# Sums of squares, products with M and scores later in TensorE's order, and a block's end as a chain of its own beside the next block's fetches

## The chip, the cores and the metric

The kernel runs on one core of a Trainium2 chip. Its engines are TensorE (PE; its weight loads are listed as PEld), VectorE (DVE), ScalarE (ACT), GpSimd (POOL), and SyncE (SP), whose work here is to issue DMAs. Each engine runs its own list of instructions in order and waits on semaphores for the others. The metric is the time of one execution on the device in microseconds (us), lower is better.

## The reference

One encoder layer over 1024 tokens of width 1024, float32, one sequence:

```
h   = modulate(rmsnorm(x))                      # scales and shifts from c
mix = gated sum of attention(h) and ssd(h)      # two token mixers, then w_out
x   = x + g1 * mix
h   = modulate(rmsnorm(x))
x   = x + g2 * peer(h)
out = rmsnorm(x) * final_norm_w
```

`ssd` is a state-space mixer in both directions, in chunks of 128 tokens, 16 heads in 2 groups. Per chunk and group its output is `M @ X` (M: 128x128 for each head, a masked product of B and C with decays) plus decayed products with the states of the chunks before (forward) and behind (backward), plus a skip term, times silu(z), followed by an rmsnorm over all 1024 channels, which needs the sum of squares of every token.

`peer` has 16384 experts. For each of 8 heads a query gives scores against two sets of 128 keys; the 16 best of each make 256 pairs, of which the 16 best are kept:

```
s1, s2 = q1 @ keys1.T, q2 @ keys2.T             # 128 scores each
idx, g = the 16 best of the 256 sums, softmax   # 8 x 16 = 128 experts per token
a      = gelu(u[idx] . h)                       # 128 rows of u for each token
y      = sum over the 128 of (g * a) * v[idx]
```

## The kernel before, in words

**The stages.** In the order of time: modulation and the first norm, the input projection, attention, the SSD mixer (its outputs from 691 to 1043 us), the gates and w_out, the second norm, the PEER queries and scores (scores from 1290 us), and from there to the end PEER itself. Matrix products are made in three passes with operands split into a high and a low part (`mm3`, lines 209 to 211): a weight slab is loaded by SP (`wr`, 3 buffers), ACT casts the high part (`wh`), POOL or DVE subtracts for the low part (`wl`), 4 buffers each.

**SSD outputs.** `outputs(c, ...)` runs for chunk c = 0 to 7, with g = 0, 1 inside. Each group goes: R matmuls (L802), exp on ACT (E), M on POOL and DVE (L806, L809, L811), the products of x with M into `y` (L815), the products dec that spread the decays over the heads (L820), those of the states (L830), DVE's sum of it all into `yt` (L832 to L843), the Square on ACT (L845), and four matmuls against ones that add the squares over channels into a bank `oq` (L849, each split into four by row in the trace). `cu`, from which M is built, lies in the same bank as `oq`. `step(FSTEP)` then issues pieces of independent projection work (matmuls of `w`), the filler between groups.

**Scores.** For each of 16 half-queries m, `query` makes q for the first 384 tokens, ACT copies it out of PSUM (L1083), and `score` multiplies it with the keys (L1093); `top` picks the 16 best on DVE.

**PEER.** The first 384 tokens (three blocks of 128) take the route by fetches: `fetched()`, a generator, yields "u" for each of 128 fetches of rows of u (POOL issues them, L1282; DVE makes the dot product with the block's rows in the double bank `gx`, L1314), then "v" for each of 128 fetches of v, which PE adds up in `gx` (L1361). `ahead` holds back the work of a fetch for some slots. The other 640 tokens take the dense route: hidden values for all experts (`hb`, weights uT), a one-hot table of the routing weights, G, built by DVE (`quad`, L1478) and PE (L1493) in pages of 64 tokens that SP stores to memory (`G_d`), then, from 2523 us, the mixing: groups of hidden values weighed with G (L1686 to L1692), multiplied with v, added to `acc` by DVE (L1722). The bank rotation `P1()` has four turns, three in `pb` and one in `io`. `gx` is one buffer (`wide()`).

**What sets the order.** In the PEER part the order of PE, DVE and POOL is written out by the program. A planner counts up estimated PE, DVE and DMA time (`at_pe`, `at_dve`, `at_dma`); after each job `feed()` steps the generator until the DMA time has caught up, and it stops at once where the generator yields "w". In the other stages a scheduler orders PE, ACT and SP by estimated times. SP's one queue issues all plain DMAs in order.

**A block's end before.** `finish` and `final` run in the generator: copy `gx` to `bacc`, take `gx` again, eight transposes into it, load x1 (512 KB) into a second `bacc` tile, of which there is one buffer, so that the load waits for the transposes; eight DVE steps (L1252), four pairs of squares on ACT (L1260) with sums on PE into `gx` (L216), the reciprocal root on DVE (L222 to L228), its spread over partitions (L237), eight DVE steps (L1271), the store. 17 times it yields "w" on the way. Only then does the next block's `begin` get `gx`.

Of the kernel before, what the change touches and what calls it, by code (L numbers as in the profile page):

```python
# [124 lines left out]
def block(ctx, tc, A, out, dbg=None):  # L125
# [490 lines left out]
    def C1():  # L616
        return psC.tile([128, 512], F32, name="pb", bufs=4 - NW)
# [149 lines left out]
    def outputs(c, xc, xk, Sf):  # L767
# [22 lines left out]
        for g in range(2):  # L790
# [9 lines left out]
            for j in range(2):  # L800
                for i, (w, r) in enumerate(R):
                    PE.matmul(o[:, j], lhsT=w, rhs=r[:, 4 * j:4 * j + 4], start=(i == 0), stop=(i == 3))  # L802
            E = ss.tile([128, 8, 128], F32, name="E")
# [8 lines left out]
            y = C1()  # L812
            for r in range(8):
                h = 8 * g + r
                PE.matmul(y[64 * (r % 2):64 * (r % 2) + 64, (r // 2) * 128:(r // 2 + 1) * 128],  # L815
                          lhsT=xk[:, h * 64:(h + 1) * 64], rhs=M[:, r], start=True, stop=True, skip_group_check=True)
# [9 lines left out]
            for d in dirs:  # L826
                st = (Sf, Sb)[d]
                for j in range(4):
                    hs = slice((8 * g + 2 * j) * 64, (8 * g + 2 * j + 2) * 64)
                    PE.matmul(of[:, d, j * 128:(j + 1) * 128], lhsT=st[:, hs], rhs=xc[:, 10 + g],  # L830
                              start=True, stop=True, skip_group_check=True)
            V.tensor_tensor(de[:, ds], of[:, ds], de[:, ds], op=OP.mult)  # L832
# [8 lines left out]
            zt = ss.tile([128, 4, 128], F32, name="zt")  # L841
# [4 lines left out]
            if g == 0:  # L846
                qr = slice(32 * (c // 2), 32 * (c // 2) + 32)
            for j in range(4):
                PE.matmul(oq[qr, :128], lhsT=one[:, 0:32], rhs=zt[:, j], start=(g == 0 and j == 0),  # L849
                          stop=(g == 1 and j == 3))  # L850
            step(FSTEP)
        ACT.copy(ysum[qr, (c % 2) * 128:(c % 2) * 128 + 128], oq[qr, :128])
# [12 lines left out]
    for c in range(8):  # L865
        xc, xk = tokens(c)
        outputs(c, xc, xk, Sf)
        if c < 7:
            Sf = advance(Sf, states(c, 0, xc, xk), c, 0)
    step(10 ** 6)  # L870
# [238 lines left out]

    norm = normed(ends[1], accs[1])  # L1110
# [127 lines left out]
    def final(p, src, t0, n, x1):  # L1238
        tl = slice(t0, t0 + n)
        def of(m):  # L1240
            o = src[:, m // 4, m % 4]
            return o if n == 128 else o.rearrange("p (g i) -> p g i", g=4)[:, :, :n // 4]

        def like(ap):
            return ap if n == 128 else ap.rearrange("p (g i) -> p g i", g=4)

        nc.sync.dma_start(x1, x1_d[:, :, tl])
        yield "w"
        yield "w"
        yield "w"  # L1250
        for m in range(8):
            V.scalar_tensor_tensor(like(x1[:, m]), of(m), mod[:, 40 + m:41 + m], like(x1[:, m]), op0=OP.mult, op1=OP.add)  # L1252
        yield "w"
        o = wide()
        acc = o[:, 0]
        for m in range(0, 8, 2):
            some = []
            for _ in range(2):
                some.append(p.tile([128, 128], F32, name="fsq", bufs=2)[:, :n])
                ACT.activation(some[-1], x1[:, m + len(some) - 1], AF.Square)  # L1260
            yield "w"
            for i, sq in enumerate(some):
                sums(sq, acc, n, m + i == 0, m + i == 7)
        yield "w"
        r = rstd(p, acc, n, 1.0 / D)
        yield "w"
        yield "w"
        yield "w"
        rb = rbcast(o[:, 1], r, n)
        for m in range(8):  # L1270
            V.scalar_tensor_tensor(x1[:, m], x1[:, m], cols[:, C_FN + m:C_FN + m + 1], rb, op0=OP.mult, op1=OP.mult)  # L1271
        nc.sync.dma_start(out[:, :, tl], x1)

    def fetched():
# [15 lines left out]
        for b in range(NB):  # L1290
            assert b in ready
            a = rt.tile([128, 128], F32, name="ba", bufs=2)
# [47 lines left out]
            for s in range(slots):  # L1340
# [5 lines left out]
                yield "u"  # L1346
            ahead.append((0, weights_of))
# [18 lines left out]
            def finish(b=b, acc=acc, n=4 * steps):  # L1366
                s = rt.tile([128, D], F32, name="bacc")
                yield "w"
                ACT.copy(v2(s), acc[0])
                yield "w"  # L1370
                yield "w"
                o = wide().rearrange("p s (m t) -> p s m t", m=4)
                for m in range(8):
                    PE.transpose(o[:, m // 4, m % 4], s[:, m * 128:(m + 1) * 128], ident)
                x1 = rt.tile([128, 1024], F32, name="bacc")[:, :8 * n].rearrange("p (m t) -> p m t", m=8)
                yield from final(rt, o, b * 128, n, x1)
# [10 lines left out]
        while ahead:  # L1387
            yield from ahead.pop(0)[1]()

# [477 lines left out]
```

## Time and profile before

| what | value |
|---|---|
| runs | 3956.99, 3949.39, 3957.73 us; median 3956.99 |
| profiled execution | 3962.2 us, its span 3960.4 us, mean granted clock 0.963 |
| busy | PE 92%, PEld 81%, DVE 65%, POOL 46%, ACT 34% of the span |
| DMA | 852.32 MB, mean 215 GB/s |
| the chain that ended last | PE 24%, DVE 5%, DMA 4% of the span, the rest in smaller shares |

The page lists the busy time of each engine, then the span in 40 slices with the busy tenths of each engine and the granted clock of PE (9: 90% or more). Waits are listed as engine, tile and line, then for whom it waited: total us, times, the longest. A line of a group names engine, operation, tile and shape, with count, busy us and mean ns behind the bar's left side, and the idle time before it with its releaser at the end. The block ends lie at about 2206 to 2310 us (block 0, while G is being placed) and 3000 to 3065 us (block 1, beside the mixing).

### The profile page before, as it was taken

The page shows a single profiled execution, that of the slowest core. Times are in us where ns is not written, and L with a number is a line of the kernel's source. Part 1 is how long each engine was busy: PE and PEld are TensorE (multiplying, and loading weights), DVE is VectorE, ACT ScalarE, POOL GpSimd, SP SyncE. Part 2 cuts the span into 40 slices and gives each one's busy share as a digit, 9 for nine tenths or more (in the row PEclk, how much of TensorE's full clock was granted, in tenths as well). Part 3 has the DMA queues.
Part 4 walks back from the last instruction along what each step waited for, and adds up shares of the span by engine and source line. Part 5 has one row for each costly group of instructions (what it writes and reads, how often), then busy time and mean ns, then how long its engine had stood idle before and what let it go on. Part 6 is the DMA issues. An engine that isn't in the chain of part 4 may idle for free. (4 is left out here: it accounts for less than half of the span.)

```text
span 3960.4 us, 61117 instructions
## 1 busy us (share of the span) xinstructions
PE 3631.6 (92%) x22927; PEld 3189.8 (81%) x22927; DVE 2574.5 (65%) x5289; ACT 1356.3 (34%) x2672; POOL 1803.3 (46%) x1526
## 2 busy tenths in 40 slices
PE   7999999988889899999889798699999999999998
PEld 4777767766679799987678698697888999888997
DVE  5788831457672678787875567594447898545556
ACT  5455532223323433322236465222122222222222
POOL 3111122566454567778775456444443444444200
PEclk9999999998899999999999899799999999999999
DMA  5111134233375258877767778888887888888632
GB/s 197 47 46 48 55 117 144 92 106 101 122 241 168 94 201 317 311 284 258 244 231 273 264 265 320 310 300 303 322 323 246 295 297 292 310 317 314 236 117 81
DMA packets 387064, 852.32 MB, mean 215 GB/s; under 512 B 32720, under 2 KB 146896, under 8 KB 384080
## 3 DMA queue, kind: packets, MB, share of 16 engines
q1 hardware_dynamic: 276176, 445.72, 32.9%
q0 software_dynamic: 110592, 402.70, 28.7%
q8 instruction: 180, 2.95, 0.3%
q14 instruction: 116, 0.95, 0.1%
HBM read 739.70 MB, written 108.59 MB: 214 GB/s over the span
## 5 line engine op out<-in xcount | busy, mean ns | idle before, releaser
L209 PE MATMUL hb<-ah,wh 128*128 128x320 f32 x2048 | 653.2, 319 | 24.0 <-ACT a L1459 24.0
L211 PE MATMUL hb<-ah,wl 128*128 128x320 f32 x2048 | 641.1, 313 | 9.7 <-POOL wl L199 9.7
L210 PE MATMUL hb<-al,wh 128*128 128x320 f32 x2048 | 639.9, 312 | 0.0
L1282 POOL DMA_INDIRECT br<-u,bidx x384 | 370.3, 964 | 369.0 <-DVE br L1314 243.2
L199 POOL TENSOR_TENSOR wl<-wr,wh 128x512 fp32r<-128x512 f32 x269 | 352.9, 1317 | 397.3 <-ACT wh L198 367.6
L209 PE MATMUL pb<-Wh,vh 128*128 128x320 f32 x1536 | 477.1, 317 | 57.1 <-ACT Wh L1689 33.7
L180 POOL TENSOR_TENSOR wl<-wr,wh 128x512 fp32r<-128x512 f32 x172 | 233.0, 1358 | 615.5 <-ACT wh L179 450.6
L1282 POOL DMA_INDIRECT br<-v,ixt x384 | 376.8, 981 | 267.5 <-PE gx L1361 155.1
L210 PE MATMUL pb<-Wl,vh 128*128 128x320 f32 x1536 | 481.4, 314 | 1.7 <-DVE Wl L1692 1.6
L211 PE MATMUL pb<-Wh,vl 128*128 128x320 f32 x1536 | 479.6, 313 | 0.0
L1314 DVE SCALAR_TENSOR_TENSOR br<-br,gx 128x1024 f32<-128x1024 f32 x384 | 454.0, 1214 | 8.6 <-DMA br<-u,bidx 6.3
L209 PEld LDWEIGHTS hb<-ah,wh 128*128 128x128 f32 x2048 | 391.9, 191 | 52.7 <-ACT a L1459 28.2
L211 PEld LDWEIGHTS hb<-ah,wl 128*128 128x128 f32 x2048 | 390.7, 191 | 11.3 <-POOL wl L199 10.3
L210 PEld LDWEIGHTS hb<-al,wh 128*128 128x128 f32 x2048 | 391.5, 191 | 0.0
L1722 DVE TENSOR_TENSOR acc<-acc,pb 128x320 f32<-128x320 f32 x491 | 230.6, 485 | 222.2 <-PE pb L211 221.0
L179 ACT CAST vh<-vr 128x512 fp32r<-128x512 f32 x256 | 151.1, 618 | 649.8 <-PE pb L210 449.0
L209 PEld LDWEIGHTS pb<-Wh,vh 128*128 128x128 f32 x1536 | 289.6, 190 | 84.4 <-ACT Wh L1689 37.0
L198 ACT CAST wh<-wr 128x512 fp32r<-128x512 f32 x288 | 178.2, 619 | 397.8 <-PE hb L210 188.2
L210 PEld LDWEIGHTS pb<-Wl,vh 128*128 128x128 f32 x1536 | 292.5, 190 | 5.4 <-DVE Wl L1692 4.3
L211 PEld LDWEIGHTS pb<-Wh,vl 128*128 128x128 f32 x1536 | 292.9, 191 | 0.4
L1478 DVE TENSOR_TENSOR quad<-io,rig 128x1024 f32<-128x1024 f32 x160 | 191.7, 1221 | 139.1 <-PE pb L1493 78.0
L180 DVE TENSOR_TENSOR vl<-vr,vh 128x512 fp32r<-128x512 f32 x256 | 203.9, 797 | 76.8 <-ACT vh L179 76.8
(367 smaller groups left out, 8218.4 us busy)
## 6 DMA issues: line engine op xcount, KB each, us to landing
wr<-uT SPq DMA_DIRECT2D x256, 256.0 KB, 3.9
vr<-v SPq DMA_DIRECT2D x256, 256.0 KB, 5.3
G_d<-stg SPq DMA_DIRECT2D x20, 2048.0 KB, 11.7
gt<-G_d SPq DMA_DIRECT2D x42, 960.0 KB, 6.5
a_d<-a SPq DMA_DIRECT2D x85, 320.0 KB, 5.3
a<-a_d SPq DMA_DIRECT2D x85, 320.0 KB, 5.9
wr<-wi SPq DMA_DIRECT2D x84, 256.0 KB, 2.7
sq<-adaT SPq DMA_DIRECT2D x32, 512.0 KB, 3.8
```

Of the source, the lines that this page charges most:

```text
L179: ACT.copy(hi, src)
L180: (eng or POOL).tensor_tensor(lo, src, f32(hi), op=OP.subtract)
L198: ACT.copy(h, raw)
L199: late.append(lambda: (eng or POOL).tensor_tensor(w, raw, f32(h), op=OP.subtract))
L209: PE.matmul(o, lhsT=wh, rhs=xh, start=first, stop=False)
L210: PE.matmul(o, lhsT=wh, rhs=xl, start=False, stop=False)
L211: PE.matmul(o, lhsT=wl, rhs=xh, start=False, stop=last)
L1282: POOL.indirect_dma_start(out=r, out_offset=None, in_=A[tab], in_offset=bass.IndirectOffsetOnAxis(ap=idx, axis=0))
L1314: V.scalar_tensor_tensor(v2(r), v2(r), 1.0, hrow[0], op0=OP.mult, op1=OP.mult, accum_out=a[:, s:s + 1])
L1478: V.tensor_tensor(x, iota.unsqueeze(1).unsqueeze(1).to_broadcast([128, 2, 4, 128]), ig[:, 0:2, t:t + 4].unsqueeze(3).to_broadcast([128, 2, ...
L1722: V.tensor_tensor(acc[:, m, js], acc[:, m, js], o, op=OP.add)
```

## The change

Four things are moved.

1. The sums of squares. After the Square on ACT, `outputs` only notes (oq, c, g, zt) in a list; `add_squares` makes the matmuls after the R matmuls of the next group, the last ones after the loop. The tile `zt` gets a second buffer. The copy of the sums moves along.
2. The products with M (`y`) come after those of dec and of the states.
3. The score of query m comes after query m+1, with its selection.
4. A block's end. `finish` copies `gx` to `bacc` and appends a generator `tail` to a list; no "w" is yielded. `tail` goes on by one piece at every third "u" of the next block, and in the last block's case at the end with a "w" each. It takes banks from `P1()` and not `gx`; x1 is loaded in two halves into `bx1`, one buffer that the squares use too; eight squares of 128x128 become two of 128x512. `ba` goes from two buffers to one.

```diff
@@ outputs @@
                     PE.matmul(o[:, j], lhsT=w, rhs=r[:, 4 * j:4 * j + 4], start=(i == 0), stop=(i == 3))
+            if squares_of:
+                add_squares()
             E = ss.tile([128, 8, 128], F32, name="E")
...
             V.tensor_tensor(M, M, E, op=OP.mult)
-            y = C1()
-            for r in range(8):
-                h = 8 * g + r
-                PE.matmul(y[...], lhsT=xk[:, h * 64:(h + 1) * 64], rhs=M[:, r], start=True, stop=True, skip_group_check=True)
             od = C2()
...
+            y = C1()
+            for r in range(8):
+                h = 8 * g + r
+                PE.matmul(y[...], lhsT=xk[:, h * 64:(h + 1) * 64], rhs=M[:, r], start=True, stop=True, skip_group_check=True)
             V.tensor_tensor(de[:, ds], of[:, ds], de[:, ds], op=OP.mult)
...
-            zt = ss.tile([128, 4, 128], F32, name="zt")
+            zt = ss.tile([128, 4, 128], F32, name="zt", bufs=2)
...
             ACT.activation(zt, yt, AF.Square)
-            if g == 0:
-                qr = slice(32 * (c // 2), 32 * (c // 2) + 32)
-            for j in range(4):
-                PE.matmul(oq[qr, :128], lhsT=one[:, 0:32], rhs=zt[:, j], start=(g == 0 and j == 0),
-                          stop=(g == 1 and j == 3))
+            squares_of.append((oq, c, g, zt))
             step(FSTEP)
-        ACT.copy(ysum[qr, (c % 2) * 128:(c % 2) * 128 + 128], oq[qr, :128])
+
+    squares_of = []
+
+    def add_squares():
+        oq, c, g, zt = squares_of.pop(0)
+        qr = slice(32 * (c // 2), 32 * (c // 2) + 32)
+        for j in range(4):
+            PE.matmul(oq[qr, :128], lhsT=one[:, 0:32], rhs=zt[:, j], start=(g == 0 and j == 0),
+                      stop=(g == 1 and j == 3))
+        if g:
+            ACT.copy(ysum[qr, (c % 2) * 128:(c % 2) * 128 + 128], oq[qr, :128])
@@ scores @@
-        s = score(m, q, range(NB))
-        for b in range(NB):
-            top(m, s[:, b], b)
+        if m:
+            tops_of(m - 1, q0)
+        q0 = q
+    tops_of(15, q0)
@@ a block's end @@
+    def half_of(b, k):
+        x = rt.tile([128, 4, 128], F32, name="bx1")
+        nc.sync.dma_start(x, x1_d[:, 4 * k:4 * k + 4, 128 * b:128 * b + 128])
+        return x
+
+    def tail(b, s, x1):
+        for k in range(2):
+            o = P1()
+            for m in range(4):
+                PE.transpose(o[:, 128 * m:128 * m + 128], s[:, 512 * k + 128 * m:512 * k + 128 * m + 128], ident)
+            for m in range(4):
+                V.scalar_tensor_tensor(s[:, 512 * k + 128 * m:512 * k + 128 * m + 128], o[:, 128 * m:128 * m + 128],
+                                       mod[:, 40 + 4 * k + m:41 + 4 * k + m], x1[:, m], op0=OP.mult, op1=OP.add)
+            if k == 0:
+                x1 = half_of(b, 1)
+            yield
+        sq = rt.tile([128, 4, 128], F32, name="bx1")
+        ACT.activation(sq.rearrange("p m t -> p (m t)"), s[:, 0:512], AF.Square)
+        yield
+        o = P1()
+        for k in range(2):
+            if k:
+                sq = rt.tile([128, 4, 128], F32, name="bx1")
+                ACT.activation(sq.rearrange("p m t -> p (m t)"), s[:, 512:1024], AF.Square)
+            for m in range(4):
+                sums(sq[:, m], o, 128, k == 0 and m == 0, k == 1 and m == 3)
+        r = rstd(rt, o, 128, 1.0 / D)
+        yield
+        rb = rbcast(P1(), r, 128)
...
+    def go_on():
+        if tails and next(tails[0], 0) == 0:
+            tails.pop(0)
...
                 yield "u"
+                if s % 3 == 2:
+                    go_on()
...
             def finish(b=b, acc=acc):
                 s = rt.tile([128, D], F32, name="bacc")
                 ACT.copy(v2(s), acc[0])
-                ...
+                tails.append(tail(b, s, half_of(b, 0)))
```

How the order moves, at three places. First TensorE in the SSD outputs, group 0 of chunk 1 and the opening of group 1 (`w` is the filler, `St` and `Sb` the forward and backward states, `kb` the spreading matrix); before:

```order
L802 MATMUL pa<-r1l,mr 128x512
L820 MATMUL pa<-dec,kb 128x128 [waits Activation_49]
L830 MATMUL pa<-xc,St 128x128 [waits Activation_49]
L815 MATMUL pb<-M,xk 64x128 [waits DVE_49]
L830 MATMUL pa<-xc,Sb 128x128 [waits DMAHW3_49]
L209 MATMUL w<-hh,wh 128x512
...
L849 MATMUL pb<-zt,ka 32x128 [waits Activation_49]
L802 MATMUL pa<-r0h,mr 128x512 [waits PE_49,Pool_49]
```

and now, up to the first products of group 1:

```order
L802 MATMUL pa<-r1l,mr 128x512
L857 MATMUL pb<-zt,ka 32x128
L817 MATMUL pa<-dec,kb 128x128 [waits Activation_49]
L827 MATMUL pa<-xc,St 128x128 [waits Activation_49]
L827 MATMUL pa<-xc,Sb 128x128 [waits DMAHW4_49]
L832 MATMUL pb<-M,xk 64x128 [waits DVE_49]
L209 MATMUL w<-hh,wh 128x512
...
L802 MATMUL pa<-r0h,mr 128x512 [waits Activation_49,Pool_49]
...
L857 MATMUL pb<-zt,ka 32x128 x4
L817 MATMUL pa<-dec,kb 128x128 [waits DVE_49]
```

The squares of group 0 (L849, now L857) stood behind the 24 filler matmuls and stand behind those and the eight R matmuls (L802); the products with M (L815, now L832) stood among those of the states and stand behind them.

Second, POOL at block 0's end, where fetches of u for block 1 (`br<-u`) meet the low parts of weights (`wl`) and the multiplication of one-hot tables (`quad`); before:

```order
L199 TENSOR_TENSOR wl<-wr,wh 128x512 [waits DMAHW1_49,PE_49,Activation_49]
L1484 TENSOR_TENSOR quad<-quad,rig 128x512 [waits DVE_49] x2
L1282 DMA br<-u,bidx 128x1024 [waits DMASW7_49]
L1282 DMA br<-u,bidx 128x1024 [waits DMASW0_49]
L1282 DMA br<-u,bidx 128x1024 [waits DMAHW3_49,DMASW1_49,Activation_49]
L1282 DMA br<-u,bidx 128x1024 [waits DMASW2_49,DVE_49]
...
L1282 DMA br<-u,bidx 128x1024 [waits DMASW5_49,DVE_49]
L199 TENSOR_TENSOR wl<-wr,wh 128x512 [waits DMAHW2_49,PE_49]
L199 TENSOR_TENSOR wl<-wr,wh 128x512 [waits DMAHW4_49,PE_49,Activation_49]
```

and now:

```order
L1503 TENSOR_TENSOR quad<-quad,rig 128x512 [waits DVE_49]
L1301 DMA br<-u,bidx 128x1024 [waits DMASW7_49]
L1301 DMA br<-u,bidx 128x1024 [waits DMASW0_49]
L199 TENSOR_TENSOR wl<-wr,wh 128x512 [waits DMAHW0_49,PE_49,Activation_49]
L199 TENSOR_TENSOR wl<-wr,wh 128x512 [waits PE_49,DMAHW2_49,Activation_49,Pool_49]
L1503 TENSOR_TENSOR quad<-quad,rig 128x512 [waits DVE_49] x2
L1301 DMA br<-u,bidx 128x1024 [waits DMAHW4_49,DMASW1_49]
L1301 DMA br<-u,bidx 128x1024 [waits DMASW2_49]
L199 TENSOR_TENSOR wl<-wr,wh 128x512 [waits DMAHW3_49,PE_49,Activation_49]
```

Before, 15 fetches stood one behind the other ahead of the next low part; now they come two at a time.

Third, DVE at the same place, where block 0's end (`bacc`) meets the one-hot tables and the dots of block 1 (`br,ba<-br,gx`); before:

```order
L1478 TENSOR_TENSOR quad<-io,rig 128x1024 [waits PE_49,Pool_49] x2
L1252 SCALAR_TENSOR_TENSOR bacc<-gx,mod,bacc 128x128 [waits DMAHW7_49]
L1478 TENSOR_TENSOR quad<-io,rig 128x1024 [waits DVE_49,PE_49,Activation_49] x2
L1478 TENSOR_TENSOR quad<-io,rig 128x1024 [waits PE_49,Pool_49]
L222 TENSOR_SCALAR rstd_32_20404<-gx 128x32 [waits PE_49]
...
L1271 SCALAR_TENSOR_TENSOR bacc<-bacc,cols,gx 128x128 [waits PE_49]
L1314 SCALAR_TENSOR_TENSOR br,ba<-br,gx 128x1024 [waits DMASW3_49,DMASW5_49,DMASW1_49,DMASW7_49,DMASW0_49,Activation_49]
```

and now:

```order
L1333 SCALAR_TENSOR_TENSOR br,ba<-br,gx 128x1024 [waits DMASW5_49,DMASW3_49,DMASW7_49,DMASW1_49,DMASW0_49]
L1497 TENSOR_TENSOR quad<-io,rig 128x1024 [waits DVE_49,PE_49,Activation_49]
L1497 TENSOR_TENSOR quad<-io,rig 128x1024 [waits PE_49,Pool_49] x2
L1266 SCALAR_TENSOR_TENSOR bacc<-pb,mod,bx_20216 128x128 [waits PE_49]
L1333 SCALAR_TENSOR_TENSOR br,ba<-br,gx 128x1024 [waits DMASW4_49,DMASW6_49,DMASW2_49,DMASW1_49]
...
L1333 SCALAR_TENSOR_TENSOR br,ba<-br,gx 128x1024 [waits DMASW3_49]
L1266 SCALAR_TENSOR_TENSOR bacc<-pb,mod,bx_20318 128x128 [waits DMAHW7_49,PE_49]
```

The dots of block 1 began behind the whole of block 0's end and now begin ahead of its first step; the steps of the end stand one set at a time between dots and one-hot tables.

More of the change, by code (lines that the diff above doesn't have):

```diff
@@ L811, in outputs @@
             V.tensor_tensor(M, M, E, op=OP.mult)
-            y = C1()
-            for r in range(8):
-                h = 8 * g + r
-                PE.matmul(y[64 * (r % 2):64 * (r % 2) + 64, (r // 2) * 128:(r // 2 + 1) * 128],
-                          lhsT=xk[:, h * 64:(h + 1) * 64], rhs=M[:, r], start=True, stop=True, skip_group_check=True)
             od = C2()
@@ L831, in outputs @@
                               start=True, stop=True, skip_group_check=True)
+            y = C1()
+            for r in range(8):
+                h = 8 * g + r
+                PE.matmul(y[64 * (r % 2):64 * (r % 2) + 64, (r // 2) * 128:(r // 2 + 1) * 128],
+                          lhsT=xk[:, h * 64:(h + 1) * 64], rhs=M[:, r], start=True, stop=True, skip_group_check=True)
             V.tensor_tensor(de[:, ds], of[:, ds], de[:, ds], op=OP.mult)
@@ L869, in block @@
             Sf = advance(Sf, states(c, 0, xc, xk), c, 0)
+    add_squares()
     step(10 ** 6)
@@ L1108, in new_q, with tops_of @@
         return sp.tile([128, S], F32, name="q", bufs=2)
+    def tops_of(m, q):
+        s = score(m, q, range(NB))
+        for b in range(NB):
+            top(m, s[:, b], b)
     norm = normed(ends[1], accs[1])
@@ L1235, in across @@
         return ig
[L1238 to L1250, printed above, removed]
-        for m in range(8):
[L1252 to L1272, printed above, removed]
@@ new lines, in block @@
+    tails = []
+    def half_of(b, k):
[26 more added lines that the diff above has]
+        rb = rbcast(P1(), r, 128)
+        for m in range(8):
+            x = s[:, m * 128:m * 128 + 128]
+            V.scalar_tensor_tensor(x, x, cols[:, C_FN + m:C_FN + m + 1], rb, op0=OP.mult, op1=OP.mult)
+        nc.sync.dma_start(out[:, :, 128 * b:128 * b + 128], s.rearrange("p (m t) -> p m t", m=8))
@@ L1291, in fetched @@
             assert b in ready
-            a = rt.tile([128, 128], F32, name="ba", bufs=2)
+            a = rt.tile([128, 128], F32, name="ba")
             ixt = rt.tile([128, 128], I32, name="ixt", bufs=2)
@@ L1364, in add, with finish @@
                 yield
-            def finish(b=b, acc=acc, n=4 * steps):
+            def finish(b=b, acc=acc):
                 s = rt.tile([128, D], F32, name="bacc")
-                yield "w"
                 ACT.copy(v2(s), acc[0])
[L1370 to L1376, printed above, removed]
+                tails.append(tail(b, s, half_of(b, 0)))
+                return
+                yield
             for i in range(steps):
@@ L1388, in fetched @@
             yield from ahead.pop(0)[1]()
+        while tails:
+            go_on()
+            yield "w"
     fetch = fetched()
```

## The prediction

> **What bounds the kernel now.** I read the page first: the busy shares, then two strips of the span in 40 slices of 99 us.
>
> ```profile
> PE 3631.6 (92%) x22927; PEld 3189.8 (81%) x22927; DVE 2574.5 (65%) x5289; ACT 1356.3 (34%) x2672; POOL 1803.3 (46%) x1526
> PE   7999999988889899999889798699999999999998
> PEclk9999999998899999999999899799999999999999
> ```
>
> TensorE (PE) is busy for 92% of the span, no other engine for more than 65%, so what PE loses is what can be won. 8% of 3960.4 us is 329 us of idle PE. Next I read the windows by stage: the SSD chunks, the score stage, block 0's end (while G is being placed), the mixing before block 1's end, that end. The columns are length, then busy time of PE, PEld, DVE, ACT, POOL, then granted clock, DMA share and GB/s.
>
> ```profile
> 700.00:1007.00 307.00, 273.58 (x1503) 211.60 (x1501) 179.27 (x269) 95.94 (x140) 184.92 (x97) 0.93 0.32 100
> 1294.00:1386.00 92.00, 77.89 (x453) 73.09 (x453) 63.41 (x376) 42.59 (x76) 50.49 (x38) 0.99 0.26 84
> 2206.00:2310.00 104.00, 79.14 (x611) 77.39 (x609) 52.71 (x78) 52.12 (x147) 49.95 (x47) 0.89 0.63 230
> 2700.00:3000.00 300.00, 299.56 (x2101) 251.88 (x2099) 147.64 (x239) 63.38 (x115) 134.09 (x131) 1.00 0.87 313
> 3000.00:3065.00 65.00, 55.58 (x396) 53.31 (x395) 50.65 (x98) 18.63 (x34) 21.46 (x21) 0.89 0.73 254
> ```
>
> Between the block ends PE has 299.56 of 300 us. PE itself paces that stretch, so a microsecond won ahead of it arrives at the end. In the touched stages it idles: 307 − 273.58 = 33.4 us, 92 − 77.89 = 14.1, 104 − 79.14 = 24.9, 65 − 55.58 = 9.4. Then the waits of PE in those windows (who waits, for whom: us in all, times, longest); the block of two rows is the score stage, which I widened to 1286 to 1387 us.
>
> ```profile
> PE pb L849 <- ACT zt L845: 18.2, 12, 3.1
> PE pb L815 <- DVE M L811: 5.6, 5, 1.9
> ...
> PE pb L1093 <- ACT q L1083: 14.1, 15, 1.0
> PE pb L1093 <- DMA keys<-keys: 3.1, 1, 3.1
> ...
> PE gx L216 <- DVE bacc L1252: 10.6, 1, 10.6
> PE hb L211 <- POOL wl L199: 9.1, 1, 9.1
> PE gx L237 <- DVE rstd L228: 1.4, 1, 1.4
> ...
> PE pb L209 <- DVE acc L1722: 7.2, 2, 5.3
> PE io L209 <- ACT Wh L1689: 2.1, 1, 2.1
> ```
>
> Nearly all the idle time has one of the change's own lines at one end of it. That is the case for a gain; what is left of each row is the question.
>
> **Parts 1 and 2: squares and y in the SSD stage.** One group of chunk 1, from the timeline:
>
> ```profile
> 754.06 1.22 DVE L832 TENSOR_TENSOR de<-pa,de 128x1024 f32<-128x1024 f32 x1 [2.57 <-PE pa L830]
> 760.40 0.63 ACT L845 ACTIVATE zt<-yt 128x512 f32<-128x512 f32 x1 [3.17 <-DVE yt L843]
> 753.95:759.55 5.60, 5.60 (x25) 1.00 0.00 0
> ```
>
> From the end of the states' products (DVE starts at 754.06) to the end of the Square (761.03) the chain takes 7.0 us, five DVE steps and an ACT step. PE had 24 matmuls of other work over it, 0.233 us each by the last row (a stretch of 5.60 us with little else), so 5.6 us, and then waited. After the change the squares of group 0 stand behind those 24 and the next eight R matmuls (8 x 0.233 = 1.9 us): 7.5 us of cover against 7.0, no wait. Those of group 1 have the next chunk's openings besides. The products with M now stand behind dec and states, 2 us and 2 us of matmuls, so most of the 5.6 us goes too.
>
> What can come back is M itself. Its build on DVE reads the bank that the squares use:
>
> ```profile
> DVE M L809 <- PE pb L849: 14.9, 6, 5.6
> 739.62 2.16 DVE L809 SCALAR_TENSOR_TENSOR M<-pb,dt,M 128x128 f32<-128x128 f32 x8 [1.74 <-POOL M L806]
> 749.10 2.40 DVE L811 TENSOR_TENSOR M<-M,E 128x1024 f32<-128x1024 f32 x1 [2.30 <-ACT E L804]
> ```
>
> Squares, then 2.16 + 2.40 = 4.6 us of DVE, then y: against about 4.1 us of dec and states and two filler matmuls (0.5). That is even, so I keep 4 us of wait in all, half a microsecond for each of eight chunks. 18.2 + 5.6 − 4 = 20 us.
>
> The clock comes on top. Two neighbouring stretches round one of the longer waits:
>
> ```profile
> 709.30:712.70 3.40, 1.44 (x10) 1.20 (x11) 1.48 (x5) 0.63 (x1) 0.00 (x0) 1.00 0.48 154
> 712.75:716.15 3.40, 3.40 (x10) 2.65 (x9) 1.84 (x8) 1.10 (x2) 1.27 (x1) 0.50 0.43 142
> ```
>
> PE idled for 2 of 3.4 us, and the next 3.4 us ran at 0.50: 1.7 us lost. The mean of the window, 0.93, puts 0.07 x 307 / 0.5 = 43 us at half clock; four such stretches follow waits of this kind, 4 x 1.7 = 6.8 us. I take 5. Ends for the parts together: 10 (the M chain costs a microsecond or more in each of the 16 groups, the clock stays) and 31 (both rows and the clock in full). Value taken: 25, since the row with the cover is nearer to the upper end.
>
> The Trainium skill, "TensorE: Matmul & The Clock Gate", section "HAM oscillation — how this bites in real kernels", gives a rule against this last term: only idle gaps of PE over about 3.4 us bring the clock down. The longest wait here is 3.1 us, so by that rule the clock term would be 0 and the sum 5 us smaller. The two rows above, 0.50 straight after a stretch with no gap that long, speak against it.
>
> **Part 3: scores.** Each of the 15 waits of 0.94 us is for one copy of a query on ACT. A query later the copy has had a whole query's matmuls (92 us for 16 queries, 5.7 us each) to end in, so all 14.1 go. The 3.1 us for the keys fall as well, since the first score comes later. Given back: the last score has nothing behind its copy (0.94), and DVE's selection, 63.41 us for 16 queries or 4.0 each, ends its last round up to one score later; I take 2.3. 17.2 − 3.2 = 14. Ends 8 and 17.
>
> **Part 4, block 0's end.** The three waits sum to 21.1 us. Their causes:
>
> ```profile
> DVE bacc L1252 <- DMA bacc<-x_d: 9.6, 1, 9.6
> L1282 POOL DMA_INDIRECT br<-u,bidx x13 | 12.2, 937 | 9.0 <-ACT gx L1309 5.1 <-issue 2.4 <-DVE br L1314 1.5
> PE pb L1493 <- ACT stg L1496: 15.1, 4, 5.4
> G_d<-stg SPq DMA_DIRECT2D x20, 2048.0 KB, 11.7
> 2231.70:2245.30 13.60, 5.00 (x35) 4.97 (x36) 4.52 (x10) 3.60 (x13) 1.04 (x1) 0.50 0.44 155
> 2269.30:2279.40 10.10, 4.00 (x15) 4.01 (x16) 6.77 (x11) 1.24 (x4) 7.34 (x7) 0.50 1.02 411
> ```
>
> The 10.6 us is PE behind sums of squares, which wait for DVE, which waits 9.6 us for x, issued only after the transposes and behind page stores of 2 MB. The 9.1 us is a low part that POOL makes late, because 13 fetches of u (0.94 us each, the window of 2257.5 to 2274) stand in a row ahead of it: fetches held back while gx was busy. Now the tail's matmuls stand every third fetch apart, the first half of x is asked for a block's end earlier, gx is free at once, and POOL's order has two fetches between low parts, not thirteen. So all three go: 21.1. PE did 5.00 + 4.00 = 9.0 us of work in these stretches at half clock, which is 4.5 us at full: worth up to 4.5 more, which I leave as the upper end. Given back: before the block's end PE waited for a stage buffer that a page store holds, four times for 15.1 us; that goes on here, 4 us once. The second half of x is asked for behind two page stores of 11.7 us each: 3 us. 21 − 7 = 14. Ends 5 and 26 (21 and the clock in full).
>
> **Part 4, block 1's end.** Two rows of waits, 9.3 us. Their cause is that block 2's dots start late and in a row, in front of DVE's additions for mixing:
>
> ```profile
> POOL br L1282 <- ACT gx L1309: 19.3, 1, 19.3
> L1314 DVE SCALAR_TENSOR_TENSOR br<-br,gx 128x1024 f32<-128x1024 f32 x16 | 18.6, 1215 | 1.1 <-ACT gx L1309 1.1
> 3065.00:3400.00 335.00, 314.04 (x2074) 306.88 (x2072) 292.66 (x526) 80.50 (x141) 140.30 (x135) 0.99 0.88 294
> 3044.10:3050.80 6.70, 5.17 (x19) 5.17 (x20) 6.70 (x10) 0.62 (x1) 5.57 (x6) 0.50 1.02 410
> 3054.30:3061.00 6.70, 4.62 (x18) 4.22 (x17) 5.73 (x9) 3.92 (x6) 1.36 (x2) 0.50 0.91 297
> ```
>
> POOL waits 19.3 us with fetches until gx carries block 2's rows; then DVE has dots of 1.2 us to catch up with, 18.6 us of 65, and PE runs 4.62 + 5.17 = 9.8 us of work at half clock (4.9 lost). With gx let go by one copy, the dots come as their rows come. I take 9.3, and 3 of the clock's 4.9. But a stretch with u fetched beside the mixing has idle time of its own: the next 335 us have 21 of it, 6%, which on 65 us is 4. 9.3 + 3 − 4 = 8. The tail's own DVE steps (2.2 us for each set of eight, L1252 and L1271 before) and copies are the same work, moved. Ends 0 and 14.
>
> **What the change adds.** The tail takes banks from the rotation of four that mixing and placing use (pb three times, io once), four turns in the tail of each of the first two blocks. A turn held means one group less in flight: PE then waits for an eviction, 2 to 3 us as in the rows of acc. I take one such wait, 3 in all, with ends 0 and 12 (each of eight turns 1.5). The two Squares of 128x512 in place of eight of 128x128 are on ACT, at 34%: nothing on the path; without that cover two at 0.63 us. zt's second buffer costs space only. Block 2's end comes behind the last fetches, beside mixing only (the last slices of the strip, all 9 but one): 0, and at most 3 either way.
>
> The Trainium skill, "Perfetto Trace Analysis", section "Matmuls", asks that independent groups of matmuls rotate through different PSUM banks so that an eviction lies beside the next group; borrowing turns works against it. It gives no price, and no run here has shown one yet.
>
> **Sum.** 25 + 14 + 14 + 8 − 3 = 58. The profiled execution took 3962.2 us (its span 3960.4 and 1.8 round it), so 3904.2; it lies 5.2 above the median of the runs shown, 3957.0, so 3899 on the runs. The ends: 10 + 8 + 5 + 0 − 12 = 11, time 3946; 31 + 17 + 26 + 14 + 0 = 88, time 3869.
>
> **Rivals.**
>
> *The squares' wait only moves.* What speaks for it: M of the next group waits for the squares' bank (14.9 us in six waits), so the later squares push M, and M pushes y, whose 16 products now stand late and have little behind them. Then the SSD parts give 6 instead of 25: 3899 + 19 = 3918. Against: the cover, 4.6 against 4.6 us, is even, not short.
>
> *Block 0's stall only moves.* x's second half lies behind the page stores, DVE's first of four steps on it waits, and behind that wait stand the quads DVE has to write for the placing; PE would wait its 10 us as before, and at block 1 the same with weights in the queue. Then the block ends give 0 instead of 22: 3921. For: 9.6 us of exactly this wait stand in the trace. Against: the first half is early, and half the load is 256 KB. Both rivals together: 3940.
>
> *The gain is swallowed.* Were the mixing paced by fetches and not by PE, what is won ahead of it would be waited for again: 3953, inside the 0.2% (8 us) that is about what a measurement of this kernel can tell from no change. Against: 299.56 of 300 us.
>
> *Slower: SP's queue is held by the tail.* SP issues in order. The second half's load now waits until DVE has read the first half, the block's store until DVE's last step, and behind them stand the weight slabs that feed PE. SP does stand waiting already:
>
> ```profile
> SPq L1472 <- ACT a L1459: 50.4, 7, 22.0
> ```
>
> It stood 22 us once without starving PE of slabs. A slab of 128x512 feeds 24 matmuls, about 3.5 us at 299.56/2101 = 0.143 us each, and three raw buffers with four split ones behind give some 7 x 3.5 = 24 us. The rival decides from holds above that: at four DMA rows of the two tails, 24 + 18 us each would cost 4 x 18 = 72 us, which eats the 61 of the gains and 11 more: 3968. Against: the longest hold in the trace is 22, and a tail's DVE steps follow their matmuls at once.
>
> *The change does not do what it says*: the scheduler could have put the moved matmuls back. The order of the built kernel excludes it.
>
> **Chances.** The forecast 0.55, the squares moved 0.12, block 0's stall moved 0.14, both 0.05, swallowed 0.08, slower 0.06. Faster is 0.55 + 0.12 + 0.14 + 0.05 = 0.86, within 0.2% 0.08, slower 0.06. The likeliest one's own range is 3879 to 3919, two of the large terms each off by ten. The range asked for reaches from the gains' upper ends, 3869, over both single rivals to 3936; it leaves out swallowed, slower and most of both together, 0.18.
>
> **What would show it.** In the profile after: PE's wait at the squares' line under 2 us in all, at y's under 5, the SSD window's mean clock over 0.95, and 33.4 us of idle there down to about 13. No wait of PE at the score line but the last. At block 0's end no row over 5 us, and fetches of u alternating with low parts on POOL; the wait of DVE for x's second half shows whether the 3 us was right. At block 1's end POOL's 19.3 gone and the clock at 1.00. It would be wrong if y waits for M in every group, if a new row of PE behind a low part or a slab appears in the first third of a block, or if the window at 2700 to 3000 shows PE under 98%.

## The result, and the profile after

The changed kernel took 3898.32 us in the median of three runs (3890.94 to 3916.14), the kernel before 3956.99. The ratio is 0.9854 with a 95% interval of 0.982 to 0.9888: 58.7 us by the medians, 44 to 71 by the interval. The forecast was 3899, 58 us. Put on a chip again beside other kernels (e4_again), the ratio was 0.9871 (0.9847 to 0.9896), 51 us. The profiled execution is the slowest of the first three, 3916.14 us with a span of 3914.3, 46 us under the profile of before; so the single stages below are read from several profiles.

The page's busy shares and the strips of PE and of its clock:

```profile
PE 3620.1 (92%) x22927; PEld 3188.2 (81%) x22927; DVE 2581.7 (66%) x5289; ACT 1351.5 (35%) x2653; POOL 1803.9 (46%) x1526
PE   6999999998789999988989898799999999999998
PEclk9999999998899999999999998899999999999999
```

Nearly the same busy time in every engine, in a shorter span. The windows for the stages of the prediction, each moved with its stage (length, busy PE, PEld, DVE, ACT, POOL, granted clock, DMA share, GB/s); the score stage's window here is 101 us long and holds the first hidden parts too:

```profile
692.00:1032.00 340.00, 296.83 (x1652) 229.17 (x1650) 207.66 (x316) 105.51 (x154) 202.23 (x106) 0.93 0.31 97
1283.00:1384.00 101.00, 93.28 (x583) 92.51 (x582) 85.65 (x487) 49.85 (x92) 62.44 (x46) 0.97 0.31 100
2160.00:2270.00 110.00, 100.73 (x770) 96.99 (x771) 63.70 (x88) 63.20 (x174) 58.58 (x55) 0.92 0.79 283
2650.00:2950.00 300.00, 298.73 (x2092) 249.47 (x2091) 143.12 (x231) 64.25 (x117) 141.74 (x139) 1.00 0.89 321
2950.00:3025.00 75.00, 67.99 (x504) 66.07 (x503) 63.30 (x119) 20.16 (x35) 23.50 (x24) 0.95 0.80 261
```

Block 0's end runs at 92% of PE where it was 76%, and the mixing before block 1's end at 298.73 of 300: what was won ahead of it arrived. The waits of PE in the SSD chunks (690 to 1000 us), the scores, block 0's end and block 1's:

```profile
PE pb L857 <- ACT zt L847: 10.1, 3, 5.6
PE w L209 <- DVE mh L677: 7.9, 2, 6.9
PE w L209 <- ACT zg L652: 6.4, 4, 2.1
PE w L210 <- DVE am L180: 4.9, 2, 4.0
PE pb L832 <- DVE M L813: 1.4, 3, 0.9
...
PE hb L209 <- ACT a L1478: 5.5, 1, 5.5
PE pb L1102 <- ACT q L1092: 2.2, 2, 1.9
PE pa L237 <- DVE rstd L228: 1.8, 1, 1.8
...
PE pb L1512 <- ACT stg L1515: 7.8, 2, 4.6
PE pb L216 <- ACT bx L1278: 1.0, 1, 1.0
...
PE io L216 <- DVE acc L1741: 5.0, 1, 5.0
PE io L209 <- ACT Wh L1708: 1.1, 1, 1.1
```

Block 0's three rows of before (10.6, 9.1 and 1.4) are gone, and of the scores' 15 waits (14.1 us) two are left (2.2). In the SSD stage the squares' row fell only from 18.2 to 10.1, and two rows of the filler grew: zg was 0.2 us before, am 2.0. The filler's gating step (mh) made PE wait 6.9 us before as well. At block 1's end a new row stands in the place of the old ones.

Where the time went, by landmarks of the trace, in us. The landmarks are instructions that every kernel has: the first R matmul, the first copy of a query, the first hidden part, the first matmul of the placing, the first weighing, the fetch of v that ends block 1, the 301st fetch of u, the last weighing.

| stage | before (two profiles) | after (two) | parts 1+2 | part 1 | part 3 | part 4 |
|---|---|---|---|---|---|---|
| SSD to first query | 596.6, 596.5 | 583.2, 578.7 | 575.2 | 579.4 | 595.8 | 596.3 |
| scores | 105.0, 103.2 | 85.5, 87.1 | 103.8 | 101.8 | 87.2 | 106.0 |
| routing, to the placing | 660.9, 659.4 | 661.4, 662.4 | 661.9 | 658.7 | 661.7 | 661.6 |
| placing with block 0's end | 469.3, 463.0 | 453.9, 457.1 | 472.4 | 469.6 | 472.7 | 458.9 |
| mixing to block 1's last v | 438.5, 443.0 | 443.0, 443.9 | 442.5 | 439.8 | 440.2 | 439.7 |
| block 1's end | 157.3, 156.3 | 153.4, 151.8 | 155.5 | 157.4 | 156.1 | 152.8 |
| rest of the mixing | 799.5, 807.4 | 799.4, 807.9 | 804.2 | 802.2 | 806.9 | 806.8 |

The last row is one reason why single executions differ: the same program spends 799 or 808 us there, with no edit near it. The first row is another: `after` and the kernel with parts 1 and 2 run the same order in this stage.

### The profile page after: what moved, and what is told of

Same layout as the page of the kernel before. It is cut to its first block, busy times and chain, and to the rows that moved or that the text cites. A ratio compares the mean times of both kernels' runs of the same rounds, so it can differ in the third digit from the quotient of the medians.

```text
span 3914.3 us, 61077 instructions
## 1 busy us (share of the span) xinstructions
PE 3620.1 (92%) x22927; PEld 3188.2 (81%) x22927; DVE 2581.7 (66%) x5289; ACT 1351.5 (35%) x2653; POOL 1803.9 (46%) x1526
## 4 chain that ended last, share of the span: by engine, by line
PE 34%; DVE 7%; DMA 7%; ACT 2%; issue 1%; POOL 1%; SPq 0%; ACTq 0%; DVEq 0%; POOLq 0%
PE pb L209 4%; PE pb L210 4%; PE pb L211 4%; DMA vr<-v 4%; PE gx L1382 4%; PE hb L209 3%; PE hb L210 3%; PE pb L1512 3%; PE hb L211 3%; DVE br L1333 2%; DMA G_d<-stg 2%; PE io L209 1%; PE io L210 1%; PE io L211 1%; DVE acc L1741 1%
## 5 line engine op out<-in xcount | busy, mean ns | idle before, releaser
L180 POOL TENSOR_TENSOR wl<-wr,wh 128x512 fp32r<-128x512 f32 x172 | 234.1, 1365 | 613.0 <-ACT wh L179 443.9
```

The costliest lines, as they stand in the source:

```text
L180: (eng or POOL).tensor_tensor(lo, src, f32(hi), op=OP.subtract)
```

## The experiments

**The parts alone.** e1_ssd has parts 1 and 2, e2_scores part 3, e3_tail part 4, each as the diff shows it, on the kernel before; e4_again is the changed kernel once more.

> The kernel before with the squares and the products with M moved (parts 1 and 2), nothing else. By the forecast 25 us are won. By the reading of the profile after, where the first score's query ends 12 us earlier and the SSD stage started 1.4 us later, 13 us. By the rival that the squares' wait only moves, 6 us or less.

> The kernel before with the scores one query later (part 3) alone. By the forecast 14 us are won. By the reading of the profile after, 18 us: the same 17 us of waits and 3.4 us of half clock at the first query, less 2 for the last selection.

> The kernel before with the block's end as a chain of its own (part 4) alone. By the forecast 14 + 8 - 3 = 19 us are won. By the reading of the profile after, 20 us at block 0's end and 4 at block 1's, less 3 to 8 that are given back between them: 16 to 21. By the rival that block 0's stall only moves, 0.

> The changed kernel once more, unchanged, for a second profile. If the parts add up, it wins as much as the three parts alone together, 45 to 60 us; if the parts disturb each other, less than their sum. The first profile of it was 18 us above the median of its runs: this one shows whether the shortfall of the SSD stage (13 us, forecast 25) belongs to that execution (then 25 here) or to the kernel (then 13 again).

Measured, as ratios to the kernel before (3972.66 us in this group): parts 1 and 2 0.9934 (0.9915 to 0.9952), 26 us; the scores 0.9943 (0.9924 to 0.9963), 23 us; the tail 0.9947 (0.9928 to 0.9965), 21 us; all together 0.9871 (0.9847 to 0.9896), 51 us. Each part is a gain of its own. Their sum is 70 us, more than the 51 of the whole; the intervals are 7 to 10 us to either side of each, 16 us for sum and whole together if they are independent, so the two stand a little further apart than these allow. (The first measurement's 44 to 71 us would still hold 70.) By the table scores and block ends are as good in the whole as alone, and only the SSD stage is longer (583.2 and 578.7 against 575.2). That is no sign of parts that disturb each other: a fourth profile of the same order in this stage, e8_late below, has 571.4. Why the whole gains less than its parts is not settled.

**The squares alone.** The first, fourth and fifth piece of the diff's part on `outputs`: squares put off, y where it was.

> The kernel before with the squares alone moved (part 1). The stage is read from its trace, from the first R matmul to the first copy of a query: 596.6 us before, 575.2 with parts 1 and 2 together. By the forecast the squares are worth 18 of the 24 us of waits and nearly all of the clock's 5, so some 578 here, with the waits for M (5.6 us) kept. If the two parts need each other (M late behind the late squares), this one gives half or less: 586 or more.

One execution, 3942.86 us beside 3966.07 of the kernel before. The stage takes 579.4 us, against 596.5: 17 us, of the 21 that parts 1 and 2 bring in their own profile. The profiles of the two orders overlap (571.4 to 583.2 with both parts), so the share of y is not fixed by this. The rows of its waits from 690 to 1045 us:

```profile
PE pb L857 <- ACT zt L847: 10.2, 4, 5.8
PE pb L817 <- DVE M L813: 10.1, 11, 3.6
```

The rival of the prediction, M pushed late by the late squares, is there: y waits 11 times where it waited six, but for 1.0 us more in all (9.1 in the same window of before). With y moved behind the states it falls to 5.6 in the whole.

**What is left of the squares' wait.** The prediction's chain from the states to the Square took 7.0 us and was taken as a constant. It is not one: in the kernel before, the same stretch in group 0 of chunk 4 takes 12.8 us (904.0 to 916.8). After the change, before the wait of 4.14 us (DVE and PE rows, then POOL in the same stretch):

```profile
892.32 7.69 DVE L842 SCALAR_TENSOR_TENSOR yt<-xc,cols,yt 128x128 f32<-128x128 f32 x4
901.45 0.76 PE L857 MATMUL pb<-zt,ka 128*32 128x128 f32 x4 [4.14 <-ACT zt L847]
892.17 1.98 POOL L796 TENSOR_TENSOR r0h<-kb,avh 128x1024 fp32r<-128x1024 f32 x1 [5.60 <-PE pa L802]
894.12 1.94 POOL L796 TENSOR_TENSOR r0l<-kb,avl 128x1024 fp32r<-128x1024 f32 x1
896.02 1.94 POOL L796 TENSOR_TENSOR r1h<-kb,avh 128x1024 fp32r<-128x1024 f32 x1
897.92 1.94 POOL L796 TENSOR_TENSOR r1l<-kb,avl 128x1024 fp32r<-128x1024 f32 x1
```

Four steps of DVE take 7.69 us, and each ends with one of the four instructions of POOL beside it. So the next edit lets these steps read y from PSUM:

```diff
-            V.tensor_tensor(ytf, y, de[:, dirs[0]], op=OP.add)
-            if len(dirs) == 2:
-                V.tensor_tensor(ytf, ytf, de[:, 1], op=OP.add)
             for j in range(4):
                 m = 4 * g + j
-                V.scalar_tensor_tensor(yt[:, j], xc[:, m], cols[...], yt[:, j], op0=OP.mult, op1=OP.add)
+                V.scalar_tensor_tensor(yt[:, j], xc[:, m], cols[...], y[:, j * 128:(j + 1) * 128],
+                                       op0=OP.mult, op1=OP.add)
+            for d in dirs:
+                V.tensor_tensor(ytf, ytf, de[:, d], op=OP.add)
```

> The changed kernel, with the skip term added first, reading y from PSUM (four steps of DVE), and then the two halves of de; same sums in another order. Theory: what is left of the squares' waits is DVE standing in steps that read and write SBUF alone, each as long as the POOL instruction beside it (0.34 us alone, up to 1.99 beside POOL's 1.9 us products); steps that read PSUM do not stretch. Then the four skip steps take 0.34 each throughout, the line's 49.7 us fall to about 22, the squares' waits of 4.1 and 5.6 us go, and the ACT copies behind the Square come earlier, so that the filler's waits of 1 to 2 us go too: the stage 5 to 10 us shorter. Rival: the steps stretch because DVE is short of something else; then they stretch here as well, and the time is that of the changed kernel.

The steps by their line, minimum, median and maximum in ns: in the changed kernel, then with the edit, where the two additions of de are the next row:

```profile
L842 DVE SCALAR_TENSOR_TENSOR yt<-xc,cols,yt x64: 339/348/1986, 707.5 to 1028.2; 128x128 f32<-128x128 f32 x64
...
L839 DVE SCALAR_TENSOR_TENSOR yt<-xc,cols,pb x64: 336/342/348, 704.0 to 1003.3; 128x128 f32<-128x128 f32 x64
L842 DVE TENSOR_TENSOR yt<-yt,de x28: 691/948/2432, 705.1 to 1003.6; 128x512 f32<-128x512 f32 x28
```

The same 64 steps never take over 348 ns when one operand is in PSUM, and up to 1986 when all are in SBUF; the steps that now read SBUF alone stretch in their place, to 2432. The changed kernel holds the same comparison without any edit, in two additions of one size, the first with y in PSUM:

```profile
L837 DVE TENSOR_TENSOR yt<-pb,de x16: 680/692/693, 706.8 to 1026.7; 128x512 f32<-128x512 f32 x16
...
L839 DVE TENSOR_TENSOR yt<-yt,de x12: 685/695/2232, 749.8 to 996.8; 128x512 f32<-128x512 f32 x12
```

So it is the operands' place that decides. The Trainium skill, "SBUF — State Buffer", section "Who interferes with whom", states it: a DVE instruction with two inputs in SBUF contends with a GpSimd instruction that reads SBUF, and the loser is blocked for the whole of it, while one with a single SBUF input does not contend. The rows agree, 1986 against 348 ns; the prediction had not used it. The stage takes 561.9 us, against 571.4 to 583.2 in the four profiles without the edit, and the squares' row to 1045 us falls from 13.7 us to 4.0, of which 3.3 stand behind the last group. The kernel is at 0.9796 (0.9783 to 0.981) of before, 81 us, clear of the changed kernel's interval.

The kernel before with this edit alone, squares and all in their old places:

> The kernel before with the skip edit alone, squares and all else as they were. By the theory that DVE's steps beside POOL's make the chain from y to the Square long, the chain gets about 2 us shorter in each group where POOL is busy, so that of the 18 us of waits at the squares some 10 go although the squares keep their place: the SSD stage 582 to 588 us instead of 597, ratio about 0.997. If the place in TensorE's order were all that counts, 595 us and no difference.

0.9961 (0.9948 to 0.9975), 15 us, and 579.2 us in the stage: as much as moving the squares. The squares still wait, more often than not, but shorter (18.2 of 12 waits before):

```profile
PE pb L849 <- ACT zt L845: 13.9, 9, 2.3
```

That row accounts for 4.3 us of the 17 that the stage gained, where some 10 were expected of it. Another 4.0 are PE's wait for a state (L764), 4.8 before and 0.8 now. The rest is seen in the window from the first R matmul to the last squares, first of the kernel before, then of this one (length, then busy PE first):

```profile
691.00:1043.10 352.10, 304.57 (x1651) 234.09 (x1648) 202.50 (x316) 108.31 (x156) 203.82 (x106) 0.90 0.30 95
690.50:1025.40 334.90, 294.47 (x1650) 226.37 (x1648) 193.98 (x316) 112.12 (x158) 206.48 (x106) 0.95 0.32 100
```

For the same matmuls PE is busy 304.6 us and 294.5, and idle 47.5 and 40.4: 10 of the 17 us are the clock, which rose from 0.90 to 0.95, 7 are waits, with the two rows above in them.

**The filler's new wait.** The four waits for zg (6.4 us) stand after the squares' old place. One of them, on ACT and PE:

```profile
845.18 0.63 ACT L847 ACTIVATE zt<-yt 128x512 f32<-128x512 f32 x1 [3.91 <-DVE yt L845]
845.71 0.60 ACT L179 CAST wh<-wr 128x512 fp32r<-128x512 f32 x1
846.22 0.58 ACT L652 COPY zg<-w 128x512 f32<-128x512 f32 x1
846.85 0.53 PE L209 MATMUL w<-hh,wh 128*128 128x512 f32 x1 [2.11 <-ACT zg L652]
```

The filler has one bank; the copy that frees it stands on ACT behind the Square, and the Square waits for DVE. PE no longer waits for the Square itself, but for what is queued behind it. With the skip edit the four waits are 4.6 us: shorter, and not gone as was expected.

**Block 0's end, data against order.** e7_oldloop has the tail's data flow (half loads, two Squares, result in bacc) in the old chain with its stops, fifteen by count where the text ahead says 17, and with gx held.

> The kernel before with only the data side of the block's end changed: x1 in two halves, the first asked for when the block's last sum starts to be copied, two Squares of 128x512, the result kept in bacc; but still one chain in the generator with its 15 stops, and gx held to its end. If the early load is what frees block 0's end, DVE's wait of 9.6 us and PE's of 10.6 go here and only POOL's 9.1 stays: 10 to 12 us from the last fetch of v of block 0 to the first weighing, 340.8 us before, 326.5 with the whole of part 4. If the chain of its own is what frees it (fetches no longer held back in a burst), nearly nothing is won here, 0 to 4. At block 1's end both expect nothing, since POOL's 19.3 us for gx stay.

From block 0's last fetch of v to the first weighing it takes 333.1 us in its one execution, against 340.8 and 335.0 in the two profiles of before and 326.5 with part 4. By itself 333.1 can't be told from 335.0; the waits say more. PE's waits there (2190 to 2300 us), DVE's for x, and PE's at the same place with part 4 whole:

```profile
PE hb L211 <- POOL wl L199: 9.1, 1, 9.1
PE gx L216 <- ACT bx L1257: 4.1, 1, 4.1
...
DVE bacc L1249 <- DMA bx<-x_d: 7.9, 1, 7.9
...
PE pb L1497 <- ACT stg L1500: 8.7, 2, 4.9
PE pb L216 <- ACT bx L1263: 3.1, 1, 3.1
```

The data side (early load, two Squares) cuts 10.6 us to 4.1; PE's wait behind POOL's burst of fetches stays at 9.1 to the tenth. In these waits both of the prediction's causes are there, one for each half of the change. And the rival's mechanism is there too: in the old chain x's second half makes DVE wait 7.9 us. In the tail it does not, as the two sets of steps stand 15 us apart and the load has that time: issued at 2205.55, used from 2220.02.

**A later tail.** The first piece at the 33rd fetch and not at the 3rd (`s % 3 == 2 and s >= 30`).

> The changed kernel with the first piece of a tail at the 33rd fetch of u of the next block and not at the 3rd. Theory: at block 1's end PE's new wait of 5.0 us is the tail's sums waiting for a bank whose last user, DVE's addition, stands behind DVE's wait for a page of G; moved away from the block's first dots the tail meets such a moment more seldom, 3 to 5 us won. Rival: it only meets another one later, and block 0's tail now runs after the page stores that it shared SP with: the same time within 3 us.

0.9841 (0.9828 to 0.9855), 63 us, beside 0.9854 and 0.9871 without: too near to be told apart. In the profile PE's waits for a stage buffer, from block 0's last v to the first weighing, fall (changed kernel, then late):

```profile
PE pb L1512 <- ACT stg L1515: 21.7, 6, 5.7
...
PE pb L1512 <- ACT stg L1515: 12.1, 3, 5.5
```

These waits repeat: 21.7 to 23.3 us in the four profiles with the early tail, 12.1 and 12.2 in the two with the late one, 15.4 in the kernel before. Placing with block 0's end takes 444.5 us here, against 453.9 and 457.1, and block 1's end 147.8 against 153.4 and 151.8. A tail that holds one of three banks when a page changes would do that; nothing here tests why. With both edits:

> The changed kernel with both edits, the skip term added first from PSUM and the tails from the 33rd fetch on. The two touch stages far apart. If they are independent: the SSD stage as with the skip edit alone (562 us, 583 and 579 in the two profiles of the changed kernel), and from block 0's last fetch of v to the first weighing as with the late tail (312 us, 318 to 328 without), a ratio to the kernel before of about 0.977. If the late tail's gain was that execution's luck, the ratio of the skip edit alone, 0.980.

0.9795 (0.9776 to 0.9815), the ratio of the skip edit alone. The stages are as expected (SSD 561.2, placing with block 0's end 440.5), but with the skip edit alone that second stage took 446.1, so that there were 6 us to win and the time shows none of it. At block 1's end, where the late tail was expected to win 3 to 5 us, the two kernels take 150.3 and 150.1. The late tail takes waits away; whether it is worth any time is open.

**The kernel before again.**

> The kernel before once more, unchanged, for a second profile: it shows how far the stages differ between two executions of the same program. The stages that no edit touches differed by 3 to 6 us among the profiles so far (the last two thirds of the mixing 952.7 to 963.0 us). Expected: the SSD stage 595 to 598, the scores 105 to 106, block 0's end 339 to 342, and the mixing up to 6 us longer than in the first profile.

3964.0 us. SSD, scores and block 1's end repeat to 2 us; placing with block 0's end came out at 463.0, 6 us shorter than in the first profile, the rest of the mixing 8 longer. Differences of single profiles below 6 to 8 us in these two stages say nothing, and in the changed order's SSD stage none below 12.

## Why the prediction was right, point by point

The sum came out within a microsecond in the first measurement and 7 us off in the second; its terms did not, so the closeness is in part luck. Its own signs show where. In the SSD chunks two failed: the squares' row was to fall under 2 us and is 10.1, and PE's 33.4 us of idle time were to fall to about 13 and are 32.3 (701 to 995 us; 23.7 in the second profile, 700 to 990). The clock at block 1's end was to be 1.00 and is 0.95. At block 0's end one row is over the 5 us named, the stage buffers' 7.8. Others held: y waits 1.4 us for M (under 5), the three old rows at block 0's end and POOL's 19.3 us at block 1's are gone, and the mixing window has 99.6% of PE (over 98).

**Squares and y: 25 forecast, 13 to 25 measured** (596.5 less 583.2, 578.7, 575.2 and, in the profile of e8_late, 571.4; the order in this stage is the same in all four). The window of the stage splits it into waits and clock, in the first and the second profile of the changed kernel and in that of e8_late:

```profile
692.30:1032.20 339.90, 296.53 (x1651) 228.91 (x1649) 207.66 (x316) 105.71 (x154) 202.23 (x106) 0.93 0.31 97
691.00:1027.00 336.00, 301.34 (x1651) 233.33 (x1649) 202.93 (x316) 105.41 (x154) 201.82 (x106) 0.92 0.31 98
689.00:1016.50 327.50, 294.93 (x1648) 229.00 (x1647) 200.19 (x316) 105.43 (x153) 202.41 (x106) 0.94 0.32 100
```

Idle time of PE fell from 47.5 to 43.4, 34.7 and 32.6 us, by 4, 13 and 15 where 20 were forecast; busy time, which is the clock's part, from 304.6 to 296.5, 301.3 and 294.9, by 8, 3 and 10 where 5 were forecast. Not all of it is the squares and y. Two rows of the kernel before for which the prediction had no term:

```profile
PE w L209 <- DVE mh L677: 6.9, 1, 6.9
PE pa L802 <- DVE St L764: 4.8, 2, 4.6
```

The wait for the gating step is 7.9 us in the first profile after and 1.0 in the other three; the wait for a state went with y's new place (5.5 us with the squares alone moved). The squares' and y's own rows to 1045 us are 21.7 and 9.1 before, 13.7 and 5.6 in the first profile, 11.5 and 5.0 in the shortest: 11 to 14 us went where 20 were forecast. So the term that was mis-sized is the waits. The step that failed is "7.5 us of cover against 7.0, no wait". The cover came out near its size, the chain did not: where the squares waited 4.1 and 5.6 us, PE had 7.4 and 6.7 us of work from the end of y to them (889.87 to 901.45, 930.94 to 944.29), and the chain from there to the end of the Square took 11.5 and 13.3, since DVE's steps on SBUF stretch beside POOL's. One group was read for a chain that has sixteen lengths. The second miss is the zg row, 6.4 us: the prediction followed who waits for the squares on PE, not what is queued behind the Square on ACT. The 4 us left for M were about right: 1.4 us to 1000 us, and 4.2 in the last chunk, where it was 3.6 before.

**The clock: 5 forecast, 3 to 10 measured.** The stage's mean rose from 0.90 to 0.92, 0.93 and 0.94, and to 0.95 with the skip edit alone. The Trainium skill, "TensorE: Matmul & The Clock Gate", section "HAM oscillation — how this bites in real kernels", gives as its rule to keep clear of idle gaps over about 3.4 us. The prediction's two rows show a fall without such a gap: PE idled 1.96 of 3.40 us, its longest wait in them was 2.2, and 0.50 followed. Longer gaps stand in the stage too (6.9 us for the gating step, 4.6 for a state), so not all of the clock's gain bears on the rule.

**Scores: 14 forecast, 16 measured** (18 in the stage, 2 given back in the next: routing takes 661.4 and 662.4 after 660.9 and 659.4). The term that was left out is the clock at the first query, in the kernel before:

```profile
1289.65:1296.40 6.75, 5.77 (x21) 5.80 (x22) 3.07 (x15) 1.93 (x3) 0.00 (x0) 0.50 0.25 96
```

5.77 us of work at half clock, 2.9 lost, behind the 3.1 us for the keys; it went with that wait. What is given back was foreseen as DVE's last selection (2.3) and shows as PE's wait of 5.5 us at the first hidden part, where before it waited 3.0.

**Block 0's end: 14 forecast, 11 measured** (466 in the mean of before's two, 455 of after's two, and 458.9 with part 4 alone; 13 by the means of the table's five profiles without part 4, 469.4, and three with it, 456.6). All three waits went. The 4 us for stage buffers were 7.8, twice and not once, each with a stretch of half clock behind it. The 3 us for x's second half were 0. The sum was nearly right by two errors of opposite sign.

**Block 1's end: 8 less the 3 for banks forecast, 4 measured.** The term for banks has its place here: PE waits 5.0 us for the bank of the tail's sums, in the second profile 1.6.

```profile
2984.24 0.82 DVE L1705 TENSOR_TENSOR a<-a,gt 128x640 f32<-128x640 f32 x1 [5.08 <-DMA gt<-G_d]
2989.45 0.66 PE L216 MATMUL io<-bx,ka 128*32 128x32 f32 x32 [4.96 <-DVE acc L1741]
```

DVE stood 5.08 us for a page of G, the addition that frees the bank stood behind it, and PE came to that bank in its turn. That is one wait in the eight turns that the tails of blocks 0 and 1 take. For the rotation rule of the Trainium skill, "Perfetto Trace Analysis", section "Matmuls", that would be a price of 1.6 to 5.0 us here, 3 forecast. But the mixing's own groups waited for the same addition before (7.2 us in two waits, one of 5.3), so how much of it the borrowed turn adds is not shown.

**The rivals.** Squares only moved: in part, with 10 us left in the squares' row to 1000 us. Block 0's stall only moved: no, but its mechanism appears as soon as the halves follow close (7.9 us). Swallowed: no, 298.73 of 300. SP's queue: SP stood for the tail's DMAs (8.2 us for DVE's first half, 7.4 for the store in 2150 to 2290 us), under the 24 that would decide, and no wait of PE is for a slab.

## What to carry to other kernels

A moved instruction is covered only if its chain keeps its length: look for the steps of the chain that another engine can stretch, and take the cover against the longest the chain shows in any group, not against one reading. Look also at what stands behind the waiting instruction on its own engine: here PE stopped waiting for the Square and began to wait for the copy behind it. And a change of order is not the only cure for a long chain: four steps per group that read PSUM in place of SBUF won 15 us alone, and with the new order the kernel is 81 us under the one before. Last, when a stage is credited with a gain, read rows that the edit did not touch as well: here one moved by 6.9 us between executions of one order.

## What was not expected of the hardware

How much this costs was not expected. DVE's steps with all operands in SBUF lasted as long as the POOL instruction beside them: 0.34 us became up to 1.99 beside POOL's 1.94 us products, and 0.69 us became up to 2.43; with one operand in PSUM the same steps kept to 0.334 to 0.349 us in 128 instructions of two kernels. The granted clock fell to 0.50 right behind a stretch of 3.4 us in which PE had idled 2 (709.30 to 716.15), so that a wait of 2.2 us cost about 1.7 more. And executions of one program differ: the kernel before by 8 us in a stretch that no edit touches (799.5 and 807.4 us), the changed order of the SSD stage by 12 (571.4 to 583.2), which none of the runs explains.
